# One PSUM bank moved from the score tiles to the transpose tiles of an attention, with a step between a row's two score tiles

## The chip, the cores and the metric

The kernel runs on one core of a Trainium2 chip. The metric is the device time of one execution in microseconds; a time given for a kernel is the median of several executions.

## The reference, cut to what matters

One layer of a hybrid encoder trunk: 1024 tokens, model width 1024, all in float32. What matters here is the stick-breaking attention: eight heads of width 64, strictly causal.

```python
def stick_breaking_attention(q, k, v):
    S = q.shape[2]
    scale = SB_HEAD_DIM ** -0.5
    ...
        z = jnp.einsum('bhqd,bhkd->bhqk', qb, kb).astype(jnp.float32) * scale
        mask = jnp.arange(t1)[None, :] < jnp.arange(t0, t1)[:, None]
        log_1mb = jnp.where(mask, jax.nn.log_sigmoid(-z), 0.0)
        tail = lax.cumsum(log_1mb, axis=3, reverse=True) - log_1mb
        attn = jnp.where(mask, jnp.exp(jax.nn.log_sigmoid(z) + tail), 0.0)
        outs.append(jnp.einsum('bhqk,bhkd->bhqd', attn.astype(vb.dtype), vb))
...
        proj = jnp.einsum('bsd,de->bse', h, w_in)
        ...
        y_pool = jnp.einsum('bsc,cd->bsd', multiscale_pool(u_pool, w_pool_mix, pool_scale), w_br_pool)
        y_sb = jnp.einsum('bsc,cd->bsd', o_sb, w_br_sb)
        gates = jax.nn.sigmoid(jnp.einsum('bsd,de->bse', h, w_gate) + b_gate)
        merged = gates[..., :D_MODEL] * y_pool + gates[..., D_MODEL:] * y_sb
        mix = jnp.einsum('bsd,de->bse', merged, w_out)
```

Around it stand an RMS norm, one input projection, the pooling mixer, and behind it a squared-ReLU MLP.

## The kernel before

Every float32 product is made of three matmuls of rounded halves: high by high, low by high, high by low (`mm3`, L110 to L112; its first matmul is L108 where it is held back behind a mark). The program runs in stages: the input and the u and v projections, the projection stage (gates, q and k, by a scheme with seven products for eight, tile name `sw`), the attention, the output projection, and the MLP.

The core's PSUM has eight banks of 128 x 512 float32. Before the change they are split by tag: two for `d` (products of dense layers), one for `o` (the attention's output), two for `z` (scores), three for `at` (transposed attention weights). The stages ahead of the attention borrow them: the u tiles take three of `at` and one of `z`, the v tiles likewise, and the projection stage's products (`newbank`) go round d, z, at.

**The attention.** The queries are worked off in two groups of 512: group 0 has query rows 3, 2, 1, 0 (each 128 queries), group 1 rows 7, 6, 5, 4, and each group runs over eight heads. For each row `att_scores` makes the scores: two matmuls into a `z` tile (L810, L813), a sigmoid on ScalarE into the row's buffer T (L815), and one scan over the row on VectorE (L817). A row of group 0 fits one tile of 512 columns or fewer; a row of group 1 needs two, which the code calls top (the columns next to the diagonal, made first) and low. `att_steps` then goes over the blocks of 128 keys of the head before, four in group 0, eight in group 1: up to four transposes of T into one `at` tile (L830), ScalarE's rounding to `ahi` (L840), VectorE's rest `alo` (L841), and, three steps later, two matmuls with v into `o` (L854). When a head's `o` is complete, ScalarE adds a bias in four pieces (`ou`, L864) and copies (`oT`, L870), and VectorE adds the two (L871).

Between all this, `pump` deals out steps of dense work on the `dbr` tiles (pooling branch, merge and output products) by a credit that each row and each attention step adds to.

**What sets the order.** The code is written in one order, and the framework's scheduler places instructions from it on each engine, by what is ready and by how many buffers a tag has. Each engine then runs its own list strictly in order. A change of the buffer counts can therefore move instructions on all engines. A tile can only be written when all readers of the tile that held the buffer before have finished.

In the projection stage `later` spreads the pooling mixer and the rearranging of v over the products. It loads v rows into `vpair` through ScalarE's DMA queue (L626), behind stores of the pooling result, and VectorE reads them at L631. The product tiles are read by VectorE at L694 to L717.

Of the kernel before, what the change touches and what calls it, by code (L numbers as in the profile page):

```python
# [19 lines left out]
F32 = mybir.dt.float32  # L20
# [12 lines left out]
P = 128  # L33
H = 512
# [18 lines left out]
class Block:  # L53
# [181 lines left out]
    def phase_in(self):  # L235
# [56 lines left out]
        for t, src in zip((self.eye, self.rcnt), self.consts):  # L292
# [7 lines left out]
            out=past, in_=past, pattern=[[1, 1024]], compare_op=ALU.is_ge, fill=0.0, base=P - 1024,  # L300
# [15 lines left out]
        for h in range(2):  # L316
# [3 lines left out]
            for k in range(NK):  # L320
                g = self.gn[:, k : k + 1]
                nc.scalar.activation(hi[:, k, :], xs[h][k], AF.Copy, scale=g)
                nc.vector.scalar_tensor_tensor(
                    out=lo[:, k, :], in0=xs[h][k], scalar=g, in1=hi[:, k, :].bitcast(F32),
# [36 lines left out]
        zu = [self.zps.tile([P, H], F32, name="zu", tag="at", bufs=3) for _ in range(3)]  # L361
        zu.append(self.zps.tile([P, H], F32, name="zu", tag="z", bufs=2))
# [77 lines left out]
        banks = [self.zps.tile([P, H], F32, name="dv", tag=t, bufs=n) for t, n in (("at", 3),) * 3 + (("z", 2),)]  # L440
# [18 lines left out]
        banks += [self.zps.tile([P, H], F32, name="dv", tag=t, bufs=n) for t, n in (("at", 3), ("z", 2))]  # L459
# [195 lines left out]
    def phase_project(self):  # L655
# [8 lines left out]
        banks = itertools.cycle([(self.dps, "d", 2), (self.zps, "z", 2), (self.zps, "at", 3)])  # L664
# [127 lines left out]
    def att_scores(self, h, i):  # L792
# [10 lines left out]
        for c, n in ((low, w - low), (0, low)):  # L803
            if n == 0:
                continue
            top = c == low
            cols = slice(c, c + max(256, n))
            z = self.zps.tile([P, H], F32, name="z", tag="z", bufs=2)
            zz = z[:, : max(256, n)]
            m = nc.tensor.matmul(zz, qq[:, 0, tt], k[:, cols], start=True, stop=False)  # L810
            if top:
                self.marks.append(m)
            nc.tensor.matmul(zz, qq[:, 1, tt], k[:, cols], start=False, stop=True)  # L813
            f = tl[:, c : c + n]
            self.after = nc.scalar.activation(f, z[:, :n], AF.Sigmoid, scale=-1.0)  # L815
        f = tl[:, :w]
# [3 lines left out]
    def att_steps(self, h, g, a):  # L820
# [3 lines left out]
        for s in range(4 * g + 4):  # L824
            r0 = max(0, s - 4 * g)
            at = self.zps.tile([P, H], F32, name="at", tag="at", bufs=3)
# [163 lines left out]
    def phase_attention(self):  # L990
# [10 lines left out]
        out = None  # L1001
        deal = [[5] * 4 + [4] * 4, [18, 18, 16, 11, 11, 11, 11, 12]]
        for g in range(2):
# [10 lines left out]
            for h in range(8):  # L1014
# [3 lines left out]
                for i in rows:  # L1018
                    a[i] = self.att_scores(h, i)
                    self.pump(rate * cost[i])  # L1020
                    if out is not None:
                        for _ in range(2 if g and h else 1):
                            next(out, None)
# [655 lines left out]
```

## Time and profile before

| | us |
|---|---|
| median of 3 executions | 1267.84 |
| lowest and highest of them | 1264.84, 1269.29 |
| the profiled execution | 1265.29 |
| its span, first to last instruction | 1263.6 |
| stage of the projections (98 to 339 us), PE busy | 237.92 of 241 |
| attention, group 0 (339 to 425 us), PE busy | 82.49 of 86 |
| attention, group 1 (425 to 568 us), PE busy | 137.20 of 143 |
| output projection's start (568 to 640 us), PE busy | 68.21 of 72 |
| from there to the end (640 to 1264 us), PE busy | 618.87 of 624 |

PE is TensorE, PEld its weight loads, DVE VectorE, ACT ScalarE, POOL GpSimd, SP SyncE. A busy matmul is counted from its issue to the end of its pipeline, so neighbours overlap; the time that a matmul costs is the distance to the start of the next. The idle time of an engine ahead of an instruction is put down to the instruction that released it last.

### The profile page before, as it was taken

To read this page: it belongs to the slowest core of one execution; us is meant where nothing else is said; L and a number is where in the kernel's file an instruction comes from. 1 tells how busy PE (TensorE), PEld (TensorE's weight loads), DVE (VectorE), ACT (ScalarE), POOL (GpSimd) and SP (SyncE) were. 2 spreads that over 40 slices of the span, in tenths; PEclk is the share of its full clock that TensorE was granted. 3 is DMA by queue.
4 is the path that set the end of the run, shared out by engine and by line. 5 is a ranking of instruction groups with operands and counts; after the bars stand their busy time and mean duration, and the time that the engine had idled before them with its cause. 6 is when DMAs were issued, how large, how long until landed. Compare 5 with 4: busy or idle time off the path is not lost.

```text
span 1263.6 us, 16163 instructions
## 1 busy us (share of the span) xinstructions
PE 1240.5 (98%) x5707; PEld 1022.1 (81%) x5707; DVE 967.1 (77%) x1311; ACT 632.0 (50%) x1010; POOL 179.5 (14%) x320
## 2 busy tenths in 40 slices
PE   9999999999999999999999999999999999999998
PEld 6887788788878887878778888888888888888887
DVE  8749887786487998868797879878865665776975
ACT  7237543344266576663566545554554433344352
POOL 2212111442001101110110012121121100001000
PEclk9999999999999999999999999999999999999999
DMA  6486896987999655454847587665559996556552
GB/s 224 157 242 177 243 273 156 319 306 242 328 337 348 175 176 150 100 165 135 286 157 249 189 282 245 221 238 208 184 193 339 299 303 228 190 196 250 199 193 68
DMA packets 110497, 283.27 MB, mean 224 GB/s; under 512 B 12496, under 2 KB 17744, under 8 KB 109264
## 3 DMA queue, kind: packets, MB, share of 16 engines
q1 hardware_dynamic: 65840, 165.41, 37.8%
q0 software_dynamic: 31040, 91.26, 25.2%
q10 hardware_dynamic: 13536, 25.57, 6.4%
q8 instruction: 45, 0.74, 0.2%
q14 instruction: 36, 0.29, 0.1%
HBM read 208.65 MB, written 94.50 MB: 240 GB/s over the span
## 4 chain that ended last, share of the span: by engine, by line
PE 70%; DVE 12%; issue 8%; DMA 7%; ACT 2%; POOL 1%; SPq 0%; ACTq 0%; DVEq 0%; POOLq 0%
PE d L111 16%; PE d L112 16%; PE d L110 16%; PE sw L110 3%; PE sw L112 3%; PE sw L111 2%; DVE T L817 2%; DMA wraw<-w 2%; PE o L854 2%; PE dbr L111 1%; PE dbr L108 1%; PE dbr L112 1%; PE at L830 1%; DVE wlo L78 1%; DVE alo L841 1%
## 5 line engine op out<-in xcount | busy, mean ns | idle before, releaser
L111 PE MATMUL d<-blo,whi 128*128 128x512 f32 (+1 forms) x456 | 172.3, 378 | 0.0
L112 PE MATMUL d<-bhi,wlo 128*128 128x512 f32 (+1 forms) x456 | 171.9, 378 | 0.0
L110 PE MATMUL d<-bhi,whi 128*128 128x512 f32 (+1 forms) x456 | 168.7, 378 | 0.0
L111 PEld LDWEIGHTS d<-blo,whi 128*128 128x128 f32 x456 | 85.7, 188 | 16.1
L112 PEld LDWEIGHTS d<-bhi,wlo 128*128 128x128 f32 x456 | 85.8, 188 | 16.0
L110 PEld LDWEIGHTS d<-bhi,whi 128*128 128x128 f32 x456 | 85.5, 188 | 15.8
L817 DVE TENSOR_TENSOR_SCAN T<-T,past 128x512 f32<-128x512 f32 (+3 forms) x64 | 84.8, 1344 | 10.5 <-ACT T L815 10.4
L111 PE MATMUL d<-b_lo,whi 128*128 128x512 f32 x196 | 76.3, 390 | 0.6 <-DVE b_lo L1105 0.6
L110 PE MATMUL d<-b_hi,whi 128*128 128x512 f32 x196 | 75.2, 390 | 1.6 <-ACT b_hi L1104 1.6
L112 PE MATMUL d<-b_hi,wlo 128*128 128x512 f32 x196 | 74.9, 390 | 0.0
L78 DVE TENSOR_TENSOR wlo<-wraw,whi 128x1024 fp32r<-128x1024 f32 x45 | 54.9, 1219 | 19.7 <-ACT whi L76 19.7
L76 ACT CAST whi<-wraw 128x1024 fp32r<-128x1024 f32 x45 | 47.4, 1053 | 43.9 <-DMA wraw<-w 18.8
L1400 ACT CAST whi<-slots_hi 128x1024 fp32r<-128x1024 f32 x29 | 30.5, 1053 | 70.2 <-PE d L111 64.0
L1402 DVE TENSOR_TENSOR wlo<-slots_hi,whi 128x1024 fp32r<-128x1024 f32 x29 | 35.5, 1224 | 38.9 <-ACT whi L1400 38.8
L1400 ACT CAST whi<-slots_lo 128x1024 fp32r<-128x1024 f32 x27 | 28.5, 1054 | 64.0 <-PE d L111 53.8
L815 ACT ACTIVATE T<-z 128x256 f32<-128x256 f32 (+2 forms) x96 | 44.8, 493 | 31.2 <-PE z L813 26.8
L110 PE MATMUL sw<-h_hi,whi 128*128 128x512 f32 x144 | 56.8, 395 | 2.7 <-DVE c L694 2.7
L111 PE MATMUL sw<-h_lo,whi 128*128 128x512 f32 x144 | 56.6, 393 | 0.0
L112 PE MATMUL sw<-h_hi,wlo 128*128 128x512 f32 x144 | 56.4, 394 | 0.0
L840 ACT CAST ahi<-at 128x512 fp32r<-128x512 f32 (+1 forms) x96 | 43.5, 483 | 25.1 <-PE at L830 23.2
L1402 DVE TENSOR_TENSOR wlo<-slots_lo,whi 128x1024 fp32r<-128x1024 f32 x27 | 33.0, 1222 | 27.3 <-ACT whi L1400 27.1
L841 DVE TENSOR_TENSOR alo<-at,ahi 128x512 fp32r<-128x512 f32 (+1 forms) x96 | 49.1, 541 | 4.9 <-ACT ahi L840 4.8
(439 smaller groups left out, 3445.7 us busy)
## 6 DMA issues: line engine op xcount, KB each, us to landing
wraw<-w SPq DMA_DIRECT2D x53, 512.0 KB, 5.1
ext_b<-ascr SPq DMA_DIRECT2D x40, 512.0 KB, 6.9
wscr<-w POOLq DMA_DIRECT2D x32, 512.0 KB, 8.8
slots_hi<-w SPq DMA_DIRECT2D x10, 1024.0 KB, 8.1
slots_lo<-w SPq DMA_DIRECT2D x10, 1024.0 KB, 8.6
qq<-qscr SPq DMA_DIRECT2D x32, 256.0 KB, 6.0
pscr<-p SPq DMA_DIRECT2D x32, 256.0 KB, 3.3
u<-pscr ACTq DMA_DIRECT2D x32, 256.0 KB, 4.4
```

The costliest lines, as they stand in the source:

```text
L76: nc.scalar.copy(hi, raw)
L78: self.lows.append(nc.vector.tensor_sub(lo, raw, hi.bitcast(F32)).ins)
L110: nc.tensor.matmul(ps, wh, rh, start=first and i == 0, stop=False)
L111: nc.tensor.matmul(ps, wh, rl, start=False, stop=False)
L112: self.last_mm = nc.tensor.matmul(ps, wl, rh, start=False, stop=last and i == n - 1).ins
L815: self.after = nc.scalar.activation(f, z[:, :n], AF.Sigmoid, scale=-1.0)
L817: nc.vector.tensor_tensor_scan(f[:, ::-1], f[:, ::-1], past[:, ::-1], 1.0, ALU.mult, ALU.max)
L840: self.att_hi = nc.scalar.copy(hi[:, c:], at[:, c:]).ins
L841: self.att_lo = nc.vector.tensor_sub(lo[:, c:], at[:, c:], hi[:, c:].bitcast(F32)).ins
L854: t = nc.tensor.matmul(o[:, c0:], v, part[:, c0:], start=s == 0 and part is hi, stop=last and part is lo)
L1400: last_split[0] = nc.scalar.copy(hi, src).ins
L1402: last_split[1] = nc.vector.tensor_sub(lo, src, hi.bitcast(F32)).ins
```

## The change

The tag `at` gets four banks and `z` one, in every place where they are used. `att_scores` takes a function `between` and calls it between a row's top and low tile. In group 1 that function makes one attention step of the head before (for the first head: half of the row's pump), and the two steps after each row become one; rows of group 0 have one tile and call nothing. The tiles of the u and v stage and the cycle of banks in the projection stage are redistributed.

```diff
-        zu = [self.zps.tile([P, H], F32, name="zu", tag="at", bufs=3) for _ in range(3)]
-        zu.append(self.zps.tile([P, H], F32, name="zu", tag="z", bufs=2))
+        zu = [self.zps.tile([P, H], F32, name="zu", tag="at", bufs=4) for _ in range(4)]
...
-        banks = [self.zps.tile([P, H], F32, name="dv", tag=t, bufs=n) for t, n in (("at", 3),) * 3 + (("z", 2),)]
+        banks = [self.zps.tile([P, H], F32, name="dv", tag=t, bufs=n) for t, n in (("at", 4),) * 3 + (("z", 1),)]
...
-        banks += [self.zps.tile([P, H], F32, name="dv", tag=t, bufs=n) for t, n in (("at", 3), ("z", 2))]
+        banks += [self.zps.tile([P, H], F32, name="dv", tag=t, bufs=n) for t, n in (("at", 4),) * 2]
...
-        banks = itertools.cycle([(self.dps, "d", 2), (self.zps, "z", 2), (self.zps, "at", 3)])
+        banks = itertools.cycle([(self.zps, "z", 1)] + [(self.zps, "at", 4), (self.dps, "d", 2)] * 2 + [(self.zps, "at", 4)] * 2)
...
-    def att_scores(self, h, i):
+    def att_scores(self, h, i, between):
...
-            z = self.zps.tile([P, H], F32, name="z", tag="z", bufs=2)
+            z = self.zps.tile([P, H], F32, name="z", tag="z", bufs=1)
...
             self.after = nc.scalar.activation(f, z[:, :n], AF.Sigmoid, scale=-1.0)
+            if top and low:
+                between()
...
-            at = self.zps.tile([P, H], F32, name="at", tag="at", bufs=3)
+            at = self.zps.tile([P, H], F32, name="at", tag="at", bufs=4)
...
                 for i in rows:
-                    a[i] = self.att_scores(h, i)
-                    self.pump(rate * cost[i])
+                    def between():
+                        if out is not None and h:
+                            next(out, None)
+                        else:
+                            self.pump(0.5 * rate * cost[i])
+
+                    a[i] = self.att_scores(h, i, between)
+                    self.pump((0.5 if g and not h else 1.0) * rate * cost[i])
                     if out is not None:
-                        for _ in range(2 if g and h else 1):
-                            next(out, None)
+                        next(out, None)
```

In the changed file the lines of `att_scores` stand one lower in number up to the sigmoid (L809, L812, L814 for L810, L813, L815), those of the transposes and behind them one higher (L831, L841, L842, L855, L865, L871), and those of the projection stage one lower (L693 for L694); the splitting of weights, L1214, is L1220.

**Group 0, between two heads, on TensorE.** These are the rows of before from the middle of the o matmuls of one head (`o_3325`) to the transposes of the next (`at_3425`); `z_3363`, `z_3389` are rows 1 and 0 of that next head, `z_3419` and `z_3443` rows 3 and 2 of the head behind it:

```order
L854 MATMUL o_3325<-alo_3370,v0_2894 128x256
L810 MATMUL z_3363<-kk_3211,qq_3210 128x256
L813 MATMUL z_3363<-kk_3211,qq_3210 128x256
L810 MATMUL z_3389<-kk_3211,qq_3210 128x256
L813 MATMUL z_3389<-kk_3211,qq_3210 128x256
L854 MATMUL o_3325<-ahi_3395,v0_2894 128x256
L810 MATMUL z_3419<-kk_3315,qq_3314 128x512
L813 MATMUL z_3419<-kk_3315,qq_3314 128x512
L854 MATMUL o_3325<-alo_3396,v0_2894 128x256
L810 MATMUL z_3443<-kk_3315,qq_3314 128x384
L813 MATMUL z_3443<-kk_3315,qq_3314 128x384
L830 MATMUL at_3425<-eye_189,T_3388 128x128
```

And the same place now:

```order
L855 MATMUL o_3325<-ahi_3395,v0_2894 128x256
L855 MATMUL o_3325<-alo_3396,v0_2894 128x256
L809 MATMUL z_3363<-kk_3211,qq_3210 128x256
L812 MATMUL z_3363<-kk_3211,qq_3210 128x256
L809 MATMUL z_3389<-kk_3211,qq_3210 128x256
L812 MATMUL z_3389<-kk_3211,qq_3210 128x256
L809 MATMUL z_3419<-kk_3315,qq_3314 128x512
L812 MATMUL z_3419<-kk_3315,qq_3314 128x512
L831 MATMUL at_3425<-eye_189,T_3388 128x128
```

All o matmuls now stand ahead of the three score tiles, which follow each other directly in the one bank; the 384 tile `z_3443` has moved behind the transposes.

On ScalarE the same place read before (`ou_3479` and `oT_3385` belong to the head `o_3325`):

```order
L815 ACTIVATE T_3362<-z_3363 128x256
L815 ACTIVATE T_3388<-z_3389 128x128
L815 ACTIVATE T_3418<-z_3419 128x512
L864 ACTIVATE ou_3479<-o_3325,vlast_197 64x128 x4
L870 COPY oT_3385<-o_3325 64x512
```

and reads now:

```order
L865 ACTIVATE ou_3479<-o_3325,vlast_197 64x128 x4
L814 ACTIVATE T_3362<-z_3363 128x256
L871 COPY oT_3385<-o_3325 64x512
L814 ACTIVATE T_3388<-z_3389 128x128
L883 CAST oh1_3487<-oT_3385 128x512
```

The sigmoid of row 1 has moved behind the four bias activations, that of row 0 behind the copy.

**Group 1, between the rows of a head, on TensorE.** These rows of the second to last head stood before around its row 4 (`z_4894` is the low tile) and the first tile of the last head (`z_4941`):

```order
L108 MATMUL dbr_4905<-mg_hi0_4046,whi_4757 128x512
L111 MATMUL dbr_4905<-mg_lo0_4047,whi_4757 128x512
L112 MATMUL dbr_4905<-mg_hi0_4046,wlo_4758 128x512
L810 MATMUL z_4894<-kk_4558,qq_4557 128x384
L813 MATMUL z_4894<-kk_4558,qq_4557 128x384
L810 MATMUL z_4941<-kk_4743,qq_4742 128x512
L813 MATMUL z_4941<-kk_4743,qq_4742 128x512
L854 MATMUL o_4767<-ahi_4859,v1_2895 128x512
L830 MATMUL at_4921<-eye_189,T_4562 128x128
```

and now (`z_4913` is row 4's low tile):

```order
L809 MATMUL z_4913<-kk_4558,qq_4557 128x384
L812 MATMUL z_4913<-kk_4558,qq_4557 128x384
L809 MATMUL z_4941<-kk_4743,qq_4742 128x512
L812 MATMUL z_4941<-kk_4743,qq_4742 128x512
L108 MATMUL dbr_4905<-mg_hi0_4050,whi_4760 128x512
L111 MATMUL dbr_4905<-mg_lo0_4051,whi_4760 128x512
L112 MATMUL dbr_4905<-mg_hi0_4050,wlo_4761 128x512
L831 MATMUL at_4946<-eye_189,T_4889 128x128
L831 MATMUL at_4946<-eye_189,T_4845 128x128
```

The two score tiles still follow each other directly; the o matmuls and transposes of the head before, which stood between the score tiles, are now done ahead of them, and the next head's transposes follow.

**The projection stage, on VectorE, at the first load of v rows.** Before:

```order
L1214 TENSOR_TENSOR wlo_1958<-wraw_1691,whi_1957 128x1024
L631 TENSOR_TENSOR vpair_1789<-vpair_1789 128x512
L694 TENSOR_TENSOR c11_1857<-u_1856,sw_1877 128x512
L707 TENSOR_TENSOR u_1856<-u_1856,sw_1908 128x512
L1214 TENSOR_TENSOR wlo_2038<-wrawx_1852,whi_2037 128x1024
L708 TENSOR_TENSOR v_1906<-u_1856,sw_1925 128x512
```

and now:

```order
L693 TENSOR_TENSOR c11_1857<-u_1856,sw_1877 128x512
L1220 TENSOR_TENSOR wlo_1958<-wraw_1691,whi_1957 128x1024
L1220 TENSOR_TENSOR s0lo_1939<-wraw_1689,s0hi_1938 128x1024
L706 TENSOR_TENSOR u_1856<-u_1856,sw_1908 128x512
L550 SCALAR_TENSOR_TENSOR qs_1899<-c11_1857,qs_1899 128x512
L630 TENSOR_TENSOR vpair_1789<-vpair_1789 128x512
L707 TENSOR_TENSOR v_1906<-u_1856,sw_1925 128x512
```

The two adds that read the product tiles `sw_1877` and `sw_1908` have moved from behind the read of the v rows to ahead of it.

## The prediction

> **What bounds the kernel now.** I read the page first, then the busy time by stage, then TensorE's waits in the two attention stages, and last the timeline around single waits.
>
> ```profile
> span 1263.6 us, 16163 instructions
> PE 1240.5 (98%) x5707; PEld 1022.1 (81%) x5707; DVE 967.1 (77%) x1311; ACT 632.0 (50%) x1010; POOL 179.5 (14%) x320
> ...
> 98.00:339.00 241.00, 237.92 (x1036) 194.54 (x1035) 186.78 (x272) 103.05 (x142) 60.91 (x98) 0.99 0.82 253
> 339.00:425.00 86.00, 82.49 (x439) 68.70 (x438) 68.44 (x103) 51.87 (x128) 8.20 (x28) 1.00 0.92 325
> 425.00:568.00 143.00, 137.20 (x730) 114.42 (x729) 122.86 (x148) 93.22 (x195) 17.83 (x36) 1.00 0.54 148
> ...
> PE at L830 <- DVE alo L841: 6.5, 6, 1.6
> PE at L830 <- DVE T L817: 1.0, 1, 1.0
> PE z L810 <- ACT T L815: 0.8, 1, 0.8
> ```
>
> TensorE is busy 98% of the span, so only its idle time can be won. In the rows by stage the columns are the stretch, its length, and busy time of PE, PEld, DVE, ACT and POOL. Query group 0 of the attention (339 to 425 us) leaves PE idle 86.00 - 82.49 = 3.5 us, group 1 (425 to 568) 143.00 - 137.20 = 5.8 us. That is 9.3 us, and 7.5 of them are waits of the transposes L830, mostly for VectorE to have read a transpose bank (alo, L841). With the score bank as it is, only one wait of 0.8 us shows. So what a fourth transpose bank can win is at most about 9 us; what matters is the price of the score bank given up.
>
> **The price of one score bank.** A score tile is two matmuls (L810, L813), then ScalarE's sigmoid (L815) reads the bank. With one bank the next tile's L810 cannot begin before that sigmoid has ended. The next rows are from the timeline (start in us, duration, engine, line; in brackets the idle time before and what ended it) and, the last three, from the groups (count | busy us, mean ns of one | idle before). They show how one such wait looks today, and how long an unhindered tile takes:
>
> ```profile
> 345.88 0.39 PE L112 MATMUL dbr<-yhi,wlo 128*128 128x512 f32 x1
> 347.06 0.39 PE L810 MATMUL z<-kk,qq 128*128 128x256 f32 x1 [0.80 <-ACT T L815]
> ...
> 348.22 0.28 PE L813 MATMUL z<-kk,qq 128*128 128x256 f32 x1
> 348.34 0.40 PE L108 MATMUL dbr<-yhi,whi 128*128 128x512 f32 x1
> ...
> 349.25 0.39 PE L813 MATMUL z<-kk,qq 128*128 128x512 f32 x1
> 349.48 0.39 PE L108 MATMUL dbr<-yhi,whi 128*128 128x512 f32 x1
> ...
> 349.68 0.60 ACT L815 ACTIVATE T<-z 128x512 f32<-128x512 f32 x1 [0.86 <-PE z L813]
> ...
> L815 ACT ACTIVATE T<-z 128x512 f32<-128x512 f32 x40 | 23.9, 600 | 22.0 <-PE z L813 18.1 <-DMA gscr<-c 3.7
> L815 ACT ACTIVATE T<-z 128x384 f32<-128x384 f32 x24 | 11.8, 492 | 4.0 <-PE z L813 3.7
> L815 ACT ACTIVATE T<-z 128x256 f32<-128x256 f32 x24 | 9.3, 388 | 4.5 <-PE z L813 4.3
> ```
>
> The sigmoid starts 349.68 - 349.25 = 0.43 us after the second matmul of a 512 tile starts and takes 0.60, so the bank is free 1.03 us after that start. For the narrower tiles I subtract what their sigmoid and matmul are shorter: 0.87 us for 384 columns, 0.70 for 256. The pitch of PE from start to start is 0.23 us for 512 columns (349.25 to 349.48), 0.12 for 256 (348.22 to 348.34) and by these about 0.17 for 384. So two tiles that follow each other directly cost a stall: 1.03 - 0.23 = 0.80 us behind a 512 tile, 0.70 behind a 384 tile, 0.58 behind a 256 tile, plus some 0.05 for the release.
>
> Now the order of the changed kernel, where the scheduler has placed the tiles. The "step" of the diff stands between the top and the low tile of a row, in group 1 alone (rows of group 0 have one tile), and nothing was put between the low tile and the top tile of the next row. I went through all 95 score tiles behind the first and summed the pitches of what stands on PE between each and the one before. In 32 places this is less than the time the bank needs, 14 in group 0 and 18 in group 1; 26 of these have next to nothing in between. The shortfalls add up to 7.6 us in group 0 and 10.8 in group 1, with the releases 18.4 + 32 x 0.05 = **20.0 us**. This is the price when ScalarE is free each time: the lower bound. In the order of before, the same sum against the tile two places back gives 0.4 us in 2 places.
>
> ScalarE is not free. In the order shown for group 0 the sigmoid of row 1 now stands behind the four bias activations ou of the head just finished (L864), and that of row 0 behind the copy oT (L870):
>
> ```profile
> 362.97 0.28 PE L854 MATMUL o<-alo,v 128*128 128x256 f32 x1
> ...
> 363.51 1.13 ACT L864 ACTIVATE ou<-o,vlast 64x128 f32<-64x128 f32 x4
> 364.65 0.58 ACT L870 COPY oT<-o 64x512 f32<-64x512 f32 x1
> ...
> L841 DVE TENSOR_TENSOR alo<-at,ahi 128x512 fp32r<-128x512 f32 x48 | 31.1, 674 | 3.7 <-ACT ahi L840 3.7
> L817 DVE TENSOR_TENSOR_SCAN T<-T,past 128x640 f32<-128x640 f32 x8 | 11.9, 1484 | 0.6 <-ACT T L815 0.5
> L840 ACT CAST ahi<-at 128x512 fp32r<-128x512 f32 x48 | 27.1, 590 | 14.3 <-PE at L830 12.9 <-issue 0.8 <-PE o L854 0.5
> ```
>
> Put in order, from the start of the last o matmul at 0: two row-1 score matmuls to 0.4; ou from 0.45 to 1.6 (1.13); row 1's sigmoid to 2.0 (0.39); row 0's matmuls at 2.05; oT to 2.55 (0.58); row 0's sigmoid to 2.8; the 512 tile of the next head from 2.85 to 3.3; then the transposes wait for row 0's scan, which VectorE does behind the add of oT, at about 3.75. In these 3.75 us PE has 0.12 + 0.24 + 0.24 + 0.45 = 1.05 of work: 2.7 us lost. The order has this boundary five times: 5 x 2.7 = 13.5. The other four short places of group 0 cost about 0.63 each, 2.5. **Group 0: 16 us.**
>
> In group 1 I went through one head of the second half in the same way: row 5's top tile stands behind the last o matmul, so its sigmoid again waits for ou and oT, and the 512 tile behind it, with three dbr matmuls (0.68 us) as its only cover, waits 1.1 us; the 256 tile behind that one 0.85 to 1.3; the next head's 512 tile behind the 384 tile 0.75; a tile before these 0.5; and the next transposes wait some 0.4 for the 640 scan (1484 ns). That is 3.6 us a head, over seven heads 25. The bound from free sigmoids is 10.8 + 18 x 0.05 = 11.7. The heads of the first half carry less on ScalarE, so I take the middle, **18 us**.
>
> **What is won.** The chains above already contain every wait that I expect in the new attention, so the 9.3 us of idle time of today go in full. The transposes run in threes now and their next use of a bank is four groups back; VectorE needs 0.67 us for one (alo), behind 0.59 of ScalarE, which the gaps of the order cover.
>
> The second gain is outside the attention. The projection's cycle of banks is now such that each bank comes round after seven products; before it was six for the tags d and z and nine for at.
>
> ```profile
> 213.73 0.87 ACTq L626 DMA_DIRECT2D vpair<-vscr  x2
> ...
> 222.13 0.39 PE L112 MATMUL sw<-h_hi,wlo 128*128 128x512 f32 x1
> 225.21 0.50 PE L110 MATMUL sw<-h_hi,whi 128*128 128x512 f32 x1 [2.69 <-DVE c L694]
> ...
> 225.78 0.62 PE L112 MATMUL sw<-h_hi,wlo 128*128 128x512 f32 x1
> ...
> 229.18 0.40 PE L111 MATMUL sw<-h_lo,whi 128*128 128x512 f32 x1
> ...
> 223.86 0.69 DVE L631 TENSOR_TENSOR vpair<-vpair 128x512 f32<-128x512 f32 x1 [3.14 <-DMA vpair<-vscr]
> 224.47 0.68 DVE L694 TENSOR_TENSOR c<-u,sw 128x512 f32<-128x512 f32 x1
> ```
>
> VectorE stood on a load of v rows until 223.86, the add L694 that frees a product bank was queued behind it, and PE lost 2.7 us. Then eight matmuls from 225.78 to 229.18 took 3.40 us instead of 8 x 0.227 = 1.82: the clock was halved for one stretch, another 1.6 us. In the new order L694 and the next product's add stand ahead of that load on VectorE; what is left behind it frees a bank that PE asks for 25 matmuls (5.7 us) later. I take 4.3 us off. If the load lands later, between 0 and 2.7 of it comes back. The input phase's v tiles still use four banks, each freed long before: nothing. The tail behind 568 us keeps its order: nothing.
>
> The Trainium skill, in "TensorE: Matmul & The Clock Gate", Part 1, says that the clock is halved after an idle window of about 3.4 us. The rows above show a halving behind a gap of 2.7 us, so the measurement is stricter than the page. By the page no boundary of the new order would halve the clock.
>
> By the row alone, the five boundaries of group 0, each idle some 2.7 us in 3.75, may halve it, at 1.6 us each. I leave these 8 us out of the sum, since gaps of up to 1.6 us in today's attention halved nothing (PEclk, the third number from the end of the stage rows, is 1.00) and the new ones come in pieces.
>
> **Sum**, against the profiled execution (1265.3 us, of which the span is 1263.6): 1265.3 + 16 + 18 - 9.3 - 4.3 = 1285.7, say **1285 us**. That execution lies 2.5 us under the median shown, 1267.84; I don't add this.
>
> **The rivals.**
> - *The score waits fall where PE would be idle anyway.* In group 1 VectorE is busy 122.86 of 143 us, so it may set the pace, and a wait for a sigmoid would only take the place of one for alo. This decides if the waits of a head stay under today's idle time, 5.8 / 8 = 0.7 us; I count 1.4 even with free sigmoids. Were it so, the time would fall by 4.3 and some of the 9.3 us, to 1252 to 1261: faster. Chance 0.08.
> - *ScalarE is always free.* 20.0 - 9.3 - 4.3 = +6.4, about 1272; with a little more hidden it lies within 0.3% of before (1264.0 to 1271.6), about what a measurement can tell from no change. Inside that band 0.09, above it is part of my forecast's range.
> - *The clock halves at the boundaries of group 0*, and the 25 us of group 1 hold: 1285 + 8 + 7 = 1300. Chance 0.10 for 1298 and more.
> - *The step does not set the tiles apart.* The order shows that it does so inside a row and not between rows; so the change does half of what it says, and the forecast already rests on this.
> - Against the direction: in "Perfetto Trace Analysis", Matmuls, the Trainium skill advises that matmul groups rotate through PSUM banks so that reading one overlaps the next group. By that rule the scores lose and the transposes gain; the wait of 0.80 us quoted above agrees for the scores.
>
> **Chances and range.** My forecast, slower by 5 to 32 us, has 0.73; with the clock case slower holds 0.83, the same 0.09, faster 0.08. The range goes from 1270 (free sigmoids, all gains, a little more hidden) to 1299 (1265.3 + 16 + 25 - 9.3 = 1297 with the projection's gain lost, and one halved clock).
>
> **What would show it.** In the changed profile: TensorE's waits of z (L809) for ACT T should be the largest, 15 to 30 us, from 0.8; those of at for alo should fall from 6.5 under 3; idle time of PE in the two attention stages should grow from 9 to 30 or 40 us and the stage become longer by as much; the 2.69 us gap with its half clock near 225 us should be gone. I am wrong if z waits stay under 10 us, which would mean that sigmoids end sooner or the tiles stand further apart than the order says; or if VectorE's alo waits remain although PE slows down.

## The result and the profile after

| | before | after |
|---|---|---|
| median of 5 executions each, taken in turn on one chip, us | 1266.59 | 1316.04 |
| lowest and highest, us | 1263.92, 1269.29 | 1315.26, 1322.1 |
| ratio after / before, with its 95% interval | | 1.0403 [1.0374, 1.0433] |
| the profiled execution, us | 1265.29 | 1315.8 |

The changed kernel is slower by 49 us. The direction was forecast, the size was not: 1285 had been predicted, with 1299 as the upper end.

The page of the changed kernel, its first rows and the granted clock by fortieths of the span:

```profile
span 1314.1 us, 16160 instructions
...
PE 1257.2 (96%) x5707; PEld 1027.4 (78%) x5707; DVE 973.4 (74%) x1311; ACT 635.0 (48%) x1010; POOL 179.1 (14%) x320
...
PEclk9999999999998999999999999999999999999999
```

The same 5707 matmuls were busy 1257.2 us, where they were busy 1240.5 before. The work has not grown; some of the same matmuls took longer. Both matter: idle time grew from 23.1 to 56.9 us (span less PE's busy time), and busy time by 16.7.

Where did it happen? The stages are cut at the same events in both kernels: from the projection stage's first product to the first score matmul, and from there to the attention's last `o`. The columns are those of the rows by stage: stretch, length, busy time of PE, PEld, DVE, ACT and POOL, granted clock, DMA share, GB/s. First before, then after; the last two rows of after split its attention into query group 0 and group 1:

```profile
98.60:339.17 240.57, 237.49 (x1034) 194.19 (x1033) 186.35 (x271) 102.45 (x141) 60.91 (x98) 0.99 0.83 254
339.17:567.20 228.03, 218.72 (x1163) 182.32 (x1162) 191.12 (x250) 144.48 (x319) 26.03 (x64) 1.00 0.68 215
```

```profile
98.90:355.10 256.20, 244.80 (x1057) 199.72 (x1056) 190.12 (x275) 103.70 (x144) 60.91 (x98) 0.99 0.82 248
355.10:618.20 263.10, 228.55 (x1139) 182.03 (x1138) 194.11 (x245) 146.61 (x316) 25.66 (x64) 0.97 0.59 178
...
355.10:441.70 86.60, 73.33 (x352) 58.53 (x350) 58.06 (x90) 44.53 (x110) 7.64 (x27) 0.92 0.79 270
441.70:618.20 176.50, 155.23 (x787) 123.50 (x788) 136.05 (x156) 102.07 (x207) 18.02 (x37) 0.99 0.49 133
```

In the changed kernel 24 dense matmuls (`dbr`) ran ahead of the first score tile instead of behind it; at 0.227 us each that is 5.4 us of work that belongs to the attention. With it put back, the projection stage is longer by 256.20 - 240.57 - 5.4 = **10 us** and the attention by 263.10 - 228.03 + 5.4 = **40 us**. What lies ahead and behind is 0.2 us shorter (span less both stages, 795.0 and 794.8). So there are two losses, and the smaller one stands where the prediction had booked a gain.

The attention's idle time is 263.10 - 228.55 = 34.5 us, from 9.3 before; the granted clock is 0.92 in group 0, where it was 1.00. TensorE's waits of the changed kernel, by releaser (total us, times, longest):

```profile
PE z L809 <- ACT T L814: 24.5, 29, 1.8
PE at L831 <- DVE T L818: 6.4, 7, 3.8
PE sw L110 <- DVE v L707: 4.4, 1, 4.4
PE dm L110 <- ACT ph L602: 2.7, 1, 2.7
...
PE o L855 <- DVE alo L842: 1.6, 2, 1.3
```

The score tiles wait for the sigmoid 29 times, 24.5 us in all, from one wait of 0.8 us before. The transposes wait no more for `alo`; now they wait for the scan (L818), whose row comes late. The third and fourth row belong to the projection stage. Each was a single wait.

One boundary between two heads of group 0, in the timeline: first PE, then ScalarE in the same 3 us.

```profile
388.56 0.28 PE L855 MATMUL o<-alo,v 128*128 128x256 f32 x1
388.68 0.28 PE L809 MATMUL z<-kk,qq 128*128 128x256 f32 x1
388.80 0.28 PE L812 MATMUL z<-kk,qq 128*128 128x256 f32 x1
390.52 0.39 PE L809 MATMUL z<-kk,qq 128*128 128x256 f32 x1 [1.45 <-ACT T L814]
390.75 0.28 PE L812 MATMUL z<-kk,qq 128*128 128x256 f32 x1
391.39 0.50 PE L809 MATMUL z<-kk,qq 128*128 128x512 f32 x1 [0.37 <-ACT T L814]
391.73 0.40 PE L812 MATMUL z<-kk,qq 128*128 128x512 f32 x1
...
388.94 1.13 ACT L865 ACTIVATE ou<-o,vlast 64x128 f32<-64x128 f32 x4 [1.31 <-PE o L855]
390.09 0.38 ACT L814 ACTIVATE T<-z 128x256 f32<-128x256 f32 x1
390.37 0.57 ACT L871 COPY oT<-o 64x512 f32<-64x512 f32 x1
391.06 0.28 ACT L814 ACTIVATE T<-z 128x128 f32<-128x128 f32 x1
```

This is the chain that the order had shown. Row 1's two score matmuls are done by 389.08, but ScalarE runs the four `ou` (388.94 to 390.07) before their sigmoid, and row 0's tile gets the bank at 390.52. The distance from 388.80 to 390.52 is 1.72 us where an undisturbed pair has 0.12, so 1.60 us are lost; the bracket shows 1.45 of them. The rest is overlap: the matmul that started at 388.80 counts as busy until 389.08, and undisturbed its neighbour would have started inside that time. The first matmul behind a wait is also slower by 0.11 us: from 390.52 to its neighbour at 390.75 it is 0.23 us where an undisturbed pair has 0.12, and from 391.39 to 391.73 it is 0.34 where 512 columns have 0.23. Idle time as recorded is less than time lost. Counted as the prediction counts, from the start of the last `o` matmul (388.56) to the first transpose (392.16), the boundary takes 3.60 us for 1.05 of work, so 2.55 are lost.

At another boundary, and at the attention's end, the changed kernel shows two things more:

```profile
378.56 0.28 PE L812 MATMUL z<-kk,qq 128*128 128x256 f32 x1
380.39 0.80 PE L809 MATMUL z<-kk,qq 128*128 128x512 f32 x1 [1.55 <-ACT T L814]
380.98 0.63 PE L812 MATMUL z<-kk,qq 128*128 128x512 f32 x1
381.41 0.63 PE L108 MATMUL dbr<-yhi,whi 128*128 128x512 f32 x1
...
602.06 0.34 PE L812 MATMUL z<-kk,qq 128*128 128x384 f32 x1
...
606.22 2.94 PE L831 MATMUL at<-eye,T 128*128 128x128 f32 x13 [3.83 <-DVE T L818]
```

Behind a wait of 1.55 us the 512-column matmuls follow each other at 0.59 and 0.43 us instead of 0.23, and last 0.63 instead of 0.39: the clock is halved for a stretch. Four such stretches stand in group 0, which is what its granted clock of 0.92 averages, and a fifth near 605 us. The length of a gap does not decide it by itself: the two waits shown at 390.52 and 391.39 us halved nothing, two of the same length at 410.14 and 411.01 did, and the longest wait for a sigmoid, 1.83 us at 469.85, did not. And behind the last head's scores no dense work is left to run. Their sigmoid starts on ScalarE only at 603.78, behind three other instructions, and the scan runs from 604.68 to 606.16, so the transposes wait 3.83 us at once.

### The profile page after: what moved, and what is told of

It is laid out like the page before. It is cut to its first block, busy times and chain, and to the rows that moved or that the text cites. A ratio compares the mean times of both kernels' runs of the same rounds, so it can differ in the third digit from the quotient of the medians.

```text
span 1314.1 us, 16160 instructions
## 1 busy us (share of the span) xinstructions
PE 1257.2 (96%) x5707; PEld 1027.4 (78%) x5707; DVE 973.4 (74%) x1311; ACT 635.0 (48%) x1010; POOL 179.1 (14%) x320
## 4 chain that ended last, share of the span: by engine, by line
PE 61%; DVE 5%; ACT 3%; DMA 2%; issue 2%; ACTq 0%; DVEq 0%; POOL 0%
PE d L112 16%; PE d L111 16%; PE d L110 16%; PE at L831 2%; PE dbr L108 2%; PE dbr L111 2%; PE o L855 2%; PE dbr L112 2%; DVE T L818 2%; PE z L809 1%; DMA wraw<-w 1%; ACT T L814 1%; PE z L812 1%; DVE wlo L78 1%; ACT ou L865 1%
## 5 line engine op out<-in xcount | busy, mean ns | idle before, releaser
L818 DVE TENSOR_TENSOR_SCAN T<-T,past 128x512 f32<-128x512 f32 (+3 forms) x64 | 86.3, 1352 | 22.5 <-ACT T L814 22.1
L814 ACT ACTIVATE T<-z 128x256 f32<-128x256 f32 (+2 forms) x96 | 47.2, 492 | 57.6 <-PE z L812 53.5
L842 DVE TENSOR_TENSOR alo<-at,ahi 128x512 fp32r<-128x512 f32 (+1 forms) x96 | 48.9, 547 | 17.5 <-ACT ahi L841 17.4
L809 PE MATMUL z<-kk,qq 128*128 128x256 f32 (+2 forms) x96 | 38.1, 397 | 24.5 <-ACT T L814 24.5
L841 ACT CAST ahi<-at 128x512 fp32r<-128x512 f32 (+1 forms) x96 | 43.4, 483 | 34.3 <-PE at L831 33.1
```

The costliest lines, as they stand in the source:

```text
L818: nc.vector.tensor_tensor_scan(f[:, ::-1], f[:, ::-1], past[:, ::-1], 1.0, ALU.mult, ALU.max)
L841: self.att_hi = nc.scalar.copy(hi[:, c:], at[:, c:]).ins
L842: self.att_lo = nc.vector.tensor_sub(lo[:, c:], at[:, c:], hi[:, c:].bitcast(F32)).ins
```

## Experiments

Each kernel ran in three rounds (e9_adds_first in five) against the kernel before on the same chip; the ratio stands with its 95% interval.

| run | what it is | median us (before beside it) | ratio |
|---|---|---|---|
| e1_attn_only | only the attention's part of the change | 1311.89 (1266.64) | 1.035 [1.0305, 1.0395] |
| e2_proj_only | only the stages ahead of the attention | 1276.54 (1266.64) | 1.0066 [1.0047, 1.0085] |
| e3_step_only | only the step between top and low tile | 1265.14 (1266.64) | 0.9987 [0.9969, 1.0005] |
| e4_banks_only | the change without the step | 1315.3 (1266.64) | 1.0367 [1.0335, 1.0399] |
| e5_at3 | e1 with three transpose banks | 1312.3 (1266.04) | 1.0357 [1.033, 1.0385] |
| e6_spaced | e1 with other work between score tiles | 1279.43 (1266.04) | 1.0107 [1.0084, 1.013] |
| e7_spaced_two_banks | the marks of e6, banks as before | 1268.92 (1266.04) | 1.0022 [1.0004, 1.0041] |
| e8_v_load_later | e2, one add ahead of the v rows' load | 1275.28 (1266.04) | 1.0073 [1.0055, 1.0091] |
| e9_adds_first | before, two adds ahead of that load | 1265.44 (1265.2) | 0.9992 [0.9977, 1.0008] |
| e10_filled | e5 with spare matmuls in the waits | 1303.62 (1265.2) | 1.0288 [1.0265, 1.0311] |
| e11_spaced_at3 | e6 with three transpose banks | 1286.58 (1265.2) | 1.016 [1.0128, 1.0193] |
| e12_d1_z2_at4 | fourth transpose bank from the dense products | 1272.82 (1266.11) | 1.0047 [1.0028, 1.0066] |

### Which part of the change costs

e1_attn_only is the kernel before with all edits of the attention, and a new split of the banks where the attention begins, so that the projection stage keeps its own:

```diff
         tc, nc = self.tc, self.nc
+        self.zps.release()
+        self.zps = tc.alloc_tile_pool(name="att_z2", bufs=1, space=PSUM, reuse_waits="tile")
...
-            z = self.zps.tile([P, H], F32, name="z", tag="z", bufs=2)
+            z = self.zps.tile([P, H], F32, name="z", tag="z", bufs=1)
...
-            at = self.zps.tile([P, H], F32, name="at", tag="at", bufs=3)
+            at = self.zps.tile([P, H], F32, name="at", tag="at", bufs=4)
```

> The attention as in the changed kernel, all stages ahead of it with the banks of before (the score and transpose pool is freed and allocated anew between the two stages). Theory, that the attention with one score bank costs 18.1 + 22.3 us by the stages of the two profiles and the projection's new cycle of banks the other 10.1: +40 us, about 1307, TensorE's z waits again near 24 us. Rival, that the projection's loss is only passed on to the attention, or the other way round: +50 or under +30.

e2_proj_only is the changed kernel with the same new split and the attention's edits undone:

```diff
+        self.zps.release()
+        self.zps = tc.alloc_tile_pool(name="att_z2", bufs=1, space=PSUM, reuse_waits="tile")
...
-            z = self.zps.tile([P, H], F32, name="z", tag="z", bufs=1)
+            z = self.zps.tile([P, H], F32, name="z", tag="z", bufs=2)
...
-            if top and low:
-                between()
...
-            at = self.zps.tile([P, H], F32, name="at", tag="at", bufs=4)
+            at = self.zps.tile([P, H], F32, name="at", tag="at", bufs=3)
```

> The stages ahead of the attention as in the changed kernel, the attention with two score and three transpose banks and no step. Theory: +10 us, about 1277, with the waits near 200 us and 331 us of the changed kernel. Rival, that the 10 us come from something of that one execution or from the attention's loads: within 4 us of before. My prediction of a gain there: -4 us.

e3_step_only is the kernel before with the step alone:

```diff
+            if top and low:
+                between()
...
-                    a[i] = self.att_scores(h, i)
-                    self.pump(rate * cost[i])
+                    a[i] = self.att_scores(h, i, between)
+                    self.pump((0.5 if g and not h else 1.0) * rate * cost[i])
```

> The kernel of before with the step between a row's two score tiles, all banks as before. Theory, that the bank and not the step costs: within 5 us of before, z waits under 3 us. Rival, that the step's bunching of transposes and output products makes the loss: +15 us or more.

e4_banks_only is the changed kernel with exactly these lines undone, so with the banks alone.

> The changed kernel without the step: one score bank and four transpose banks, two attention steps behind each row as before. Theory: as slow as the changed kernel or a little slower, +45 to +60 us (by the order 31 score tiles are too close, as in the changed kernel), z waits 22 us or more. Rival, that the step costs: +30 us or less.

The attention's part costs 45.3 us, the stages ahead of it 9.9. The two make 55 where the whole change makes 49; the interval of e1's ratio alone is about 6 us to either side, so an overlap of the two parts is not shown. The new split was not run by itself, so what it costs inside e1 and e2 is not separated; the stages of the changed kernel, which does without it, give 40 and 10. The step alone is worth nothing that can be measured, and without it the banks cost the same 49 us. So it neither harms nor protects: e4's score tiles wait 26.1 us, against 24.5 with the step.

```profile
PE z L809 <- ACT T L814: 26.1, 29, 2.0
```

The two single waits of the projection stage are in e2 too, where the attention has the banks of before:

```profile
PE sw L110 <- DVE v L707: 4.0, 1, 4.0
PE dm L110 <- ACT ph L602: 2.5, 1, 2.5
```

### Which of the two bank counts, and the order of the tiles

e5_at3 gives the eighth bank to nobody:

```diff
-            at = self.zps.tile([P, H], F32, name="at", tag="at", bufs=4)
+            at = self.zps.tile([P, H], F32, name="at", tag="at", bufs=3)
```

> The run with the attention's part alone (1312), but with three transpose banks, so that the eighth bank stays empty in the attention: the price of the score bank with nothing got for it. By the order 28 score tiles stand too close instead of 31, with 15.5 us short instead of 18.5. Theory, that the fourth bank is worth little because the wait for the scores gives VectorE the time to free three: within 5 us of 1312, transposes waiting for alo under 4 us. Rival, that it is worth the 6.5 to 9 us that it was meant to win: 1318 to 1321.

e6_spaced is e1 with dense work between the score tiles. Each dense product is held behind a mark some places back, and only top tiles, transposes and `o` matmuls were marks. Now low tiles are, too, and the distance is two:

```diff
-LAG = 4
+LAG = 2
...
-            if top:
-                self.marks.append(m)
+            self.marks.append(m)
```

By the order, 14 tiles now come too early for the one bank, by 2.3 us in sum, where e1 has 31 tiles and 18.5 us.

> The run with the attention's part alone, with the dense steps held back behind the second to last mark instead of the fourth to last (LAG 2 for 4), and each low score tile a mark as well. The order then has 14 score tiles too close, by 2.3 us in all, instead of 31 by 18.5. Theory, that the loss is the score tiles standing next to each other on TensorE: z waits under 10 us from 23, few half-clock stretches in the attention, 1280 to 1292. Rival, that one score bank costs by its depth wherever the tiles stand, since ScalarE is late anyway: over 1302.

e7_spaced_two_banks is the control: e3_step_only with the same three lines, so that scores have two banks and transposes three. The scheduler does not place it in the very order of e6; what the two have in common is the spacing. In both traces 3 of the 95 later score tiles follow the one before directly, where e1 has 24.

> The control of the spaced run: the kernel of before with the step, two score banks and three transpose banks, and the same LAG of 2 and marks on low tiles. It tells what that other order costs by itself. Theory: 0 to 10 us over before (dense work held back leaves less to fill the waits of the transposes), so the spaced run stands 10 us or more above it by its ScalarE waits and no more than 25. Rival, that holding back is free: same as before, 1265.

e11_spaced_at3 is e6 with the edit of e5.

> The spaced run (1279.4) with three transpose banks and the eighth bank empty: the worth of the fourth transpose bank where score waits are short. Theory, from the two unspaced runs (1311.9 and 1312.3): worth under 4 us, 1278 to 1283. Rival, that the fourth bank is worth its 6.5 us here, where less idle time gives VectorE relief: 1285 or more, with waits for alo over 5 us.

e5 is as slow as e1 (1312.3 and 1311.9, each known to about 4 to 6 us): while the score tiles hold TensorE up, no gain from the fourth transpose bank can be seen. e5's order has three tight tiles fewer, which may hide a small one. e6 is 32.5 us faster than e1 with the same banks; the order of the score tiles carries most of the loss. What is left for the exchange of banks is e6 against its control, 1279.4 - 1268.9 = 10.5 us. For the score bank by itself, with nothing got for it, it is e11 against the same control: 1286.6 - 1268.9 = 17.7 us. e6's largest wait is still 10.1 us, where the order alone gave 2.3; what else delays the sigmoids there was not followed up. Its row, then those of e7 and of e11, each from TensorE's waits:

```profile
PE z L810 <- ACT T L814: 10.1, 13, 1.7
```

```profile
PE at L831 <- DVE alo L842: 3.2, 5, 0.9
...
PE z L810 <- ACT T L814: 0.5, 2, 0.3
```

```profile
PE z L810 <- ACT T L814: 8.9, 14, 1.3
PE at L831 <- DVE alo L842: 3.2, 5, 1.8
```

With the score waits short, the transpose bank seems to count. e11 without it is 7 us slower than e6, against other runs of before; the ratios' intervals just touch (1.013 and 1.0128), so the sign is likely rather than certain. The expectation for it had been under 4 us. Waits for `alo` of 3.2 us came back, less than the rival's 5; e11's profiled execution also has half-clock stretches near 585 and 626 us that e6's has not, so not all of the 7 us are such waits.

### The half clock

e10_filled is e5 with spare matmuls (58, ahead of 26 score tiles that come too early, one to three each) into the empty bank. Each runs behind the score tile before and ahead of the next; what they write is not used.

```diff
+            for _ in range(FILL.get(self.n_z, 0)):
+                spare = self.zps.tile([P, H], F32, name="spare", tag="spare", bufs=1)
+                with self.behind(last):
+                    last = nc.tensor.matmul(spare, qq[:, 0, tt], k[:, :H], start=True, stop=True).ins
...
+            with self.behind(last):
+                m = nc.tensor.matmul(zz, qq[:, 0, tt], k[:, cols], start=True, stop=False)
```

> The run with three transpose banks and one empty bank (1312), with spare matmuls of 512 columns between score tiles that stand too close, 58 in all, one to three where the wait is long enough, 13.1 us of TensorE work; what they write into the empty bank is not used. They lie inside the waits for the sigmoid, so they cost at most what a wait is shorter than they are. Theory, that the half-clock stretches (seven in the attention of that run) come from the idle time: at most three are left and the time falls by 4 to 8 us, to 1304 to 1308. Rival, that they depend on something else: seven again, and 1312 to 1320.

Work was added and the time fell, 1312.3 to 1303.6. The attention by stage, e5 and then e10:

```profile
343.70:613.10 269.40, 236.20 (x1150) 187.80 (x1148) 195.11 (x246) 147.05 (x317) 25.77 (x64) 0.95 0.58 178
```

```profile
341.60:603.00 261.40, 245.04 (x1208) 191.73 (x1207) 194.72 (x246) 145.89 (x316) 25.75 (x64) 0.99 0.58 182
```

58 matmuls more, 8.0 us less, and the granted clock rises from 0.95 to 0.99: seven stretches of half clock became two. One of the seven is twice as long as the others, so at some 1.6 us a stretch five or six of them make 8 to 10 us, which is the size of the gain. The placed order of e10 differs from e5's in a few more places than the spare matmuls, so the figure is not exact to the microsecond. A wait of this length therefore costs itself and, in some places where several stand close, the clock behind it.

### The projection stage

In the changed kernel the gap at 222 us is gone as forecast. Two others have come. From the timeline of after, PE and then VectorE:

```profile
199.97 0.39 PE L112 MATMUL sw<-ht_hi,a1lo 128*128 128x512 f32 x1
203.10 0.79 PE L110 MATMUL dm<-ph,wm 128*128 128x512 f32 x1 [2.74 <-ACT ph L602]
...
330.93 0.39 PE L112 MATMUL sw<-ht_hi,s1lo 128*128 128x512 f32 x1
335.76 0.66 PE L110 MATMUL sw<-ht_hi,whi 128*128 128x512 f32 x1 [4.45 <-DVE v L707]
336.22 0.63 PE L111 MATMUL sw<-ht_lo,whi 128*128 128x512 f32 x1
...
325.50 0.68 DVE L706 TENSOR_TENSOR u<-u,sw 128x512 f32<-128x512 f32 x1
332.95 0.69 DVE L630 TENSOR_TENSOR vpair<-vpair 128x512 f32<-128x512 f32 x1 [6.78 <-DMA vpair<-vscr]
334.94 0.68 DVE L707 TENSOR_TENSOR v<-u,sw 128x512 f32<-128x512 f32 x1
```

It is the pattern that before had near 222 us, at the last load of v rows instead of the first: VectorE stands 6.78 us on the load, the add L707 that frees a product bank is queued behind it, and PE waits 4.45 us and goes on at half clock. In the kernel before, that add (L708, at 317.23 us) stood ahead of the read of the last load (L631, at 321.31). Over the whole stage VectorE waits 21.2 us for v rows in 7 places, where it was 12.8 us in 6. The other gap, at 203.10, waits for ScalarE's `ph`, which starts when VectorE's sum for the pooling (`win`, L598, at 201.80) is done; no run tried to take it away.

e8_v_load_later takes that add out of the queue. It is e2 with the last read of v rows held behind the add; PE's order stays.

```diff
+            while t == 7 and self.v_add is None:
+                yield
...
+            with self.behind(self.v_add if t == 7 else None):
+                nc.vector.tensor_sub(e, e, p[:, 1, :])
...
+            add = nc.vector.tensor_add(v, u, product(w["sa"], 0, "t3")).ins
+            if i == len(self.PAIRS) - 2:
+                self.v_add = add
```

> The run with the projection's part alone (1276.5), with one change of order on VectorE: the add that reads the last loaded v rows stands behind the add v of the product, not ahead of it; TensorE's order is the same. Theory, that VectorE stood on this load with the product's add queued behind it, 4.0 us of idle TensorE and one half-clock stretch of 1.6: -5 us, about 1271, the half clock near 333 us gone. Rival, that the wait passes to the next instruction behind the load: unchanged, 1275 to 1278.

By the medians it won 1.3 us, by the ratios nothing (1.0073 against 1.0066), so no gain is shown. The add stands ahead now, but VectorE still stands on the same load and the next reader of a bank is the one that is late. From e8's timeline, VectorE and then PE:

```profile
326.89 0.69 DVE L711 TENSOR_TENSOR v<-u,sw 128x512 f32<-128x512 f32 x1
332.78 0.69 DVE L634 TENSOR_TENSOR vpair<-vpair 128x512 f32<-128x512 f32 x1 [5.20 <-DMA vpair<-vscr]
...
336.10 0.80 PE L111 MATMUL sw<-h_hi,whi 128*128 128x512 f32 x1 [2.00 <-DVE u L716]
```

e9_adds_first asks for the gain that the prediction had booked, in the kernel before itself: the two adds of pair 5 that stood behind the first load of v rows are put ahead of it, with nothing else changed.

```diff
+            while t == 0 and self.u_add is None:
+                yield
...
+            with self.behind(self.u_add if t == 0 else None):
+                nc.vector.tensor_sub(e, e, p[:, 1, :])
...
+            add = nc.vector.tensor_add(u, u, product(w["sb"], 0, "t2")).ins
+            if i == 5:
+                self.u_add = add
```

> The kernel of before, with the two product adds ahead of the first read of loaded v rows on VectorE, as the changed kernel has them; TensorE's order and all banks as before. It tries the step of the prediction that took 4.3 us off. Theory, that the adds of the product were what TensorE missed: the 2.7 us gap near 222 us and its half-clock stretch of 1.6 us are gone, 1262, ratio 0.9965. Rival, that the next instruction behind the load takes the wait over, as in the run with the last load read later: 1264 to 1267.

The gap at 222 us went, and the time stayed (0.9992 [0.9977, 1.0008]). VectorE's timeline there shows the add ahead of the load and only 1.25 us stood on it, where it was 3.14:

```profile
221.93 0.69 DVE L711 TENSOR_TENSOR u<-u,sw 128x512 f32<-128x512 f32 x1
223.87 0.69 DVE L635 TENSOR_TENSOR vpair<-vpair 128x512 f32<-128x512 f32 x1 [1.25 <-DMA vpair<-vscr]
```

TensorE's waits of e9 have a new row in the same stage:

```profile
PE sw L111 <- DVE u L723: 2.4, 2, 1.2
```

These two waits stand at 255.36 and 297.53 us. Ahead of the first, VectorE stands 5.21 us on the third load of v rows (until 253.41), with the add L723 queued behind it: the same pattern at a later load. The second has no load ahead of it. This profiled execution is the slowest of the twelve (1271.02 us), so its rows can name the waits but not their price; the median says that nothing was won. So the 4.3 us were not there to be won by freeing one bank earlier. What sets the pace of this stage (the landing of the v rows, or VectorE's chain behind it) was not settled: no run changed the loads themselves.

### Another place to take the bank from

e12_d1_z2_at4 leaves the scores two banks and takes the transposes' fourth from the dense products during the attention:

```diff
+        self.zps.release()
+        self.dps.release()
+        self.dps = tc.alloc_tile_pool(name="att_d1", bufs=1, space=PSUM, reuse_waits="tile")
+        self.zps = tc.alloc_tile_pool(name="att_z2", bufs=1, space=PSUM, reuse_waits="tile")
...
-            at = self.zps.tile([P, H], F32, name="at", tag="at", bufs=3)
+            at = self.zps.tile([P, H], F32, name="at", tag="at", bufs=4)
```

> The kernel of before with four transpose banks and two score banks in the attention; the bank is taken from the dense products there (d, one instead of two). No step. It asks whether the fourth transpose bank is worth its 7.5 us of waits when the scores keep theirs. Theory: waits of the transposes for alo fall from 6.5 us to under 2, and a dense product now waits for VectorE to have read the one before, some 1 us for those of the 31 that no attention work separates: 1265 to 1280. Rival, that dense products always have other work between them: faster than before, 1258 to 1261.

It costs 6.7 us. The transposes' waits for `alo` are gone from its list, and others have come: for the loads of a head's k, which land too late for a score tile, and for the readers of the one dense bank. Waits for k of 1.2, 4.5 and 2.6 us also stand in e3, e6 and e7, so they go with the order and not with the dense bank alone.

```profile
PE z L810 <- DMA kk<-qscr: 5.5, 4, 2.4
...
PE dbr L108 <- DVE gm L946: 1.7, 2, 1.0
```

None of these versions is faster than the kernel before by more than its interval.

## Why the prediction was wrong in size

Forecast were +20.4 us (16 + 18 - 9.3 - 4.3), measured +49.5. By its steps:

- **The price of one score bank, as waits: right in sum.** z waits were to be 15 to 30 us and are 24.5; the attention's idle time was to be 30 to 40 us and is 34.5, near the 16 + 18 of the two groups. By groups it is 13.3 (86.60 - 73.33) and 21.3 (176.50 - 155.23), so that the sum fits so well is in part luck: two misses of some 3 us cancel. The `at` waits for `alo` were to fall below 3 and are gone (an `o` matmul has 1.6). e4 and e3 put it on the banks and not on the step. The group 0 boundary that was worked out at 2.7 us lost measured 2.55 in the rows above.
- **Free sigmoids as the lower bound, the sigmoid behind `ou` as the reason for more: right.** The boundary's rows show the sigmoid in that place. The rival in which the waits fall where PE is idle anyway is out, since the attention grew by 40 us.
- **"I leave these 8 us out of the sum": failed.** Halved clocks stand behind waits of up to 1.55 us in group 0 (clock 0.92), and e10 wins 8 us by filling the waits. With the stretch at the attention's end there are five, some 8 us, the very sum left out; that it fits is luck in part, since the prediction had them all at the five boundaries of group 0, and one of those boundaries, at 390.52, halved nothing. The row of the prediction, a halving behind 2.7 us, had pointed there; the reason given against it, that today's gaps of up to 1.6 us halved nothing, was about single gaps. The rule cited there from the Trainium skill, "TensorE: Matmul & The Clock Gate", Part 1 (a halving after an idle window of about 3.4 us), would by itself have given none of the four in group 0, where no gap is longer than 1.55 us. The trace does not agree with it as the only rule, and the prediction's "no boundary of the new order would halve the clock" had taken it as that.
- **Recorded idle time taken for time lost: failed, a size.** The attention's idle time grew by 25.2 us, but its length by 40. The 15 us between are busy time of the same matmuls. By an estimate from the rows above, five half-clock stretches at some 1.6 us are 8 of them, and 29 waits that each cost some 0.15 us of overlap and 0.11 us for the slower first matmul are 7 to 8.
- **"The next transposes wait some 0.4 for the 640 scan", in each head of group 1: too small at the end.** The last head's wait was 3.83 us, since no dense work was left beside it and its sigmoid stood behind other work on ScalarE.
- **"I take 4.3 us off" for the projections: failed, in sign.** The mechanism was seen rightly at one place and taken for the stage. e2 measures +9.9 for the stages ahead of the attention. Their largest new wait is the same queueing at the last load of v rows, where the add now stands behind the read instead of ahead of it; but e8, which puts it ahead again, wins nothing that is clear of noise, so which of the new waits sets the 9.9 stays open. e9 shows that even with the banks of before the gap at 222 us was no gain: it went, and the median stayed. The bound "between 0 and 2.7 of it comes back" had only looked at this one load; seven others and the stage's end were not looked through.

The miss of 29 us is thus 45.3 - 24.7 = 20.6 in the attention and 9.9 + 4.3 = 14.2 ahead of it, less the 6 by which the two runs of parts together exceed the whole.

## What to carry to other kernels

Before a bank is moved from one use to another, sum over the new order what stands between each tile and the one that frees its bank, and put the reading engine's own queue into that sum; here the bank given up cost 46 us with adjacent tiles (e5) and some 18 with other work between them (e11 against e7), while the bank gained was worth nothing that could be measured in the first order and some 7 us in the second. Do not book a visible wait as a gain until the next user of the same engine has been followed: of the wait removed in the projections nothing measurable arrived, in two kernels (e8 and e9). Where waits will cluster, add the clock's loss to them.

## What the runs showed of the hardware that was not expected

- The clock halved behind short gaps: behind 1.55 us at 380.4, where another wait stood close ahead, as well as behind 2.74 and 4.45 us in the projections. It did not do so each time: waits of 1.45 and 0.37 us halved it at 410.14 and 411.01 us and not at 390.52 and 391.39. Spare matmuls in such gaps raised the granted clock of the stage from 0.95 to 0.99.
- A wait costs more than the bracket shows: at 388.80 to 390.52 us 1.60 lost for 1.45 recorded, at 378.56 to 380.39 us 1.71 for 1.55, since the overlap with the matmul before is lost with it; the first matmul behind the wait takes 0.11 us more on top.
